# Hybrid three-branch layer: half of a projection's finishing work moved behind the next half, gate tiles in buffers of their own, branch weights asked for earlier

## The chip, the cores and the metric

The kernel runs on one core of one Trainium2 chip. The metric is device time in microseconds (us) of one execution; the median of three runs is taken. TensorE does the matrix products, VectorE (DVE), ScalarE (ACT) and GpSimd (POOL) do the elementwise work, SyncE (SP) and GpSimd issue transfers. Each engine works off its own list of instructions strictly in order, so an instruction that waits holds up everything behind it on its engine, and a transfer that waits in SP's list holds up all later transfers of that list.

## The reference

The layer works on x (1024 rows, width 1024) and 256 memory tokens. After a norm, one wide projection of h gives the inputs of three token mixers (A: top-256 sparse attention, B: low-rank attention, M: attention into the memory), three gate paths z and three merge gates. What matters here is the end of it:

```python
ys = jnp.stack([o_a * jax.nn.silu(z_a), o_b * jax.nn.silu(z_b), o_m * jax.nn.silu(z_m)], axis=0)
branch = jnp.einsum('nbsw,nwd->nbsd', ys, w_branch[layer])
gates = jax.nn.sigmoid(gate_logits)
merged = jnp.einsum('bsnd,nbsd->bsd', gates, branch)
x = x + merged @ w_out[layer]
```

and, for mixer A, the projections q_a, k_a, v_a with a per-head norm and rotary embedding.

## The kernel before

Every product of two fp32 matrices is done as three TensorE products (`mm3`: high by high, high by low, low by high), where high is the operand rounded for TensorE and low the remainder. So each weight block is loaded raw (one transfer on SP's list), its high part is cast on ScalarE and its low part subtracted on VectorE (`wload` and `wsplit`).

The order in time is: memory attention, B's attention, the indexer of A, then branch 2 (M), branch 1 (B), the last projections for A, A's attention, branch 0 (A) and the output projection. A search for the 256th largest index value of each row (`topk_group`; its operations are named `ka..` and `kd..`) is cut into small steps that `run_topk` puts between other work on ScalarE and VectorE, from the indexer to just before A's attention.

`branch(n, ...)` has a first part that makes `y` = mixer output times silu(z), and a merge loop over 8 blocks `d` of 128 output columns, each with two halves `j` of 512 rows: 16 half tiles of 12 matmuls. A half tile needs the block's weights (`b{n}w{d}`), a stored gate tile `tg` (tanh of half the gate logit, computed earlier, stored in HBM and loaded here), and a PSUM bank (names `br`), taken in turn from a group of two and a group of three banks. `emit` then merges: for branches 2 and 1 one VectorE instruction (tg + 1) * br into a tile `ac` (named `ab` for branch 2, `am` for branch 1), which POOL's list sends to HBM, for branch 1 as an accumulating transfer. For branch 0, `emit_a` multiplies, adds the sum from HBM on POOL, casts the high part on ScalarE (`hTh`) and subtracts the low part on VectorE (`hTl`), the inputs of the output projection, whose weights are `wo`.

Between the two parts of branches 2 and 1 stands `qkv(p)` (`mid`): the q, k and v projection of two heads, in two halves `j` of four row blocks each (names `a_0..` and `a_1..`). Per half, the results are copied from PSUM, squared and summed (`ss`), POOL turns the sums into factors (`rr`), VectorE applies rotary, POOL multiplies q and k by the factors, q is split, and q, k, v are stored.

In the phase of branches 2 and 1 the tiles xq, xk, xv, their squares, `tg` and `ac` all come in turn from one pool tag `t2k` with nine buffers; weight tiles share two raw buffers and seven split ones:

```python
return wk.tile([P, 512], F32, tag="t2k", name=nm, bufs=9)
```

A scheduler turns the program into the engines' lists; a buffer's next user waits for its last reader.

Of the kernel before, what the change touches and what calls it, by code (L numbers as in the profile page):

```python
# [11 lines left out]
F32 = mybir.dt.float32  # L12
# [9 lines left out]
S = 1024  # L22
D = 1024
P = 128
# [17 lines left out]
NZG = 3  # L42
WSF = [1]
WSO = [1]
WOD = (1, 1)
ZB5 = 4
OB5 = 4
PRF = (2, 2)
# [47 lines left out]
def f(ap):  # L96
    return ap.bitcast(F32)
# [3 lines left out]
def hybrid_kernel(  # L101
# [922 lines left out]
    def topk_group(ts, nm, act):  # L1024
# [56 lines left out]
        if act:  # L1081
            up = tk.tile([P, nb], F32, name=nm + "u")
            for i, t in enumerate(ts):
                n = (t + 1) * P
                sg = sign(i, t)
                big = tk.tile([P, S], BF, tag="tke", name=f"{nm}b{t}", bufs=1)[:, 0:n]
                nc.vector.tensor_scalar(out=big, in0=sg, scalar1=0.5, scalar2=-GONE, op0=ALU.is_le, op1=ALU.mult)
                y = tk2[0].tile([P, S], F32, tag="tks", name=f"{nm}y{t}", bufs=1)[:, 0:n]
                nc.vector.tensor_tensor_reduce(out=y, in0=idx[t], in1=big, op0=ALU.add, op1=ALU.min, scale=1.0,
                                               scalar=-GONE, accum_out=up[:, i:i + 1])  # L1090
                yield n / 480 + 0.2
            nc.vector.tensor_scalar(out=cnt, in0=cnt, scalar1=TOPK - 0.5, scalar2=None, op0=ALU.is_gt)
            nc.vector.tensor_tensor(up, up, cnt, op=ALU.mult)
            nc.vector.tensor_scalar(out=cnt, in0=cnt, scalar1=-1.0, scalar2=1.0, op0=ALU.mult, op1=ALU.add)
            nc.vector.tensor_tensor(T, T, cnt, op=ALU.mult)
            nc.vector.tensor_tensor(T, T, up, op=ALU.subtract)
            fix[0] = 1
        else:
            nT = tk.tile([P, nb], F32, name=nm + "m")
            nc.vector.tensor_scalar(out=nT, in0=T, scalar1=-1.0, scalar2=None, op0=ALU.mult)  # L1100
# [181 lines left out]
            bg(zi[0], 5.1)  # L1282
        z_done.add((n, w))

    def branch(n, zc, wpool, wk, yp, o_T, emit, bg=None, tgb=9, wkt=None, zb=2, ob=2, mid=None, tgt="t2k"):

        yh, yl, b0 = [None] * 4, [None] * 4, None

        def b_weights(d):
            return wload(wpool, f"b{n}w{d}", [(wview(w_branch[n], 0, 4, d * P, P), P)], 4, P, wkind[1])  # L1290

        early_z = {}
        if n == 0:
            for w in range(4):
                if (n, w) not in z_done:
                    early_z[w] = z_part(n, w, zc, wpool, wk, zb)
            b0 = b_weights(0)
# [36 lines left out]
    with w3s as ph:  # L1334
# [3 lines left out]
        wk = ph.enter_context(tc.tile_pool(name="gwork", bufs=2, reuse_waits="tile"))  # L1338

        def t2k(nm):  # L1340
            return wk.tile([P, 512], F32, tag="t2k", name=nm, bufs=9)

        def acc_at(d, j):
            return s_acc[d * P:(d + 1) * P, j * 512:(j + 1) * 512]

        def emit_b(d, j, tg, pb):
            ac = t2k(f"ab{d}_{j}")
            i_ = nc.vector.scalar_tensor_tensor(out=ac, in0=tg, scalar=1.0, in1=pb, op0=ALU.add, op1=ALU.mult)
            nc.gpsimd.dma_start(acc_at(d, j), ac)
            run_topk(i_, 2.6)  # L1350

        def emit_m(d, j, tg, pb):
            ac = t2k(f"am{d}_{j}")
            i_ = nc.vector.scalar_tensor_tensor(out=ac, in0=tg, scalar=1.0, in1=pb, op0=ALU.add, op1=ALU.mult)
            nc.gpsimd.dma_start(acc_at(d, j), ac, accum_op=ALU.add)
            run_topk(i_, 2.6)

        def qkv(p):
# [9 lines left out]
            for j in range(2):  # L1368
# [8 lines left out]
                for i in range(4):  # L1377
# [7 lines left out]
                    for e, x_ in enumerate((xq, xk, xv)):  # L1385
                        i_ = nc.scalar.copy(x_[:, i], psv[:, e])
                    run_topk(i_, 4.2)
                for e, x_ in enumerate((xk, xq)):
                    sq = t2k(f"{nm}sq{e}").rearrange("p (t d) -> p t d", t=8)
                    nc.scalar.activation(sq, x_.rearrange("p t h d -> p (t h) d"), AF.Square)  # L1390
                    nc.vector.tensor_reduce(out=ss[:, e, :], in_=sq, op=ALU.add, axis=AX.X)  # L1391
                    nc.vector.tensor_tensor(x_.rearrange("p t h d -> p (t h) d"), x_.rearrange("p t h d -> p (t h) d"),
                                            g_am[:, 1 - e:2 - e, :].to_broadcast([P, 8, 64]), op=ALU.mult)
                rsqrt_mean(rr, ss, 1.0 / 64)
                nc.gpsimd.tensor_scalar(out=rr[:, 1, :], in0=rr[:, 1, :], scalar1=64 ** -0.5,
                                        scalar2=0.0, op0=ALU.mult, op1=ALU.add)
                for e, x_ in enumerate((xk, xq)):
                    rope(x_[:, :, :, 0:16], cos_a[:, b, :], sin_a[:, b, :], 2, 8, wk, f"ar{p}_{j}_{e}")
                    r_ = rr[:, e, :].rearrange("p (t h) -> p t h", t=4).unsqueeze(3).to_broadcast([P, 4, 2, 64])
                    nc.gpsimd.tensor_tensor(x_, x_, r_, op=ALU.mult)  # L1400
                nc.scalar.copy(vst[:, :, 0::3, :], xv)
                nc.vector.tensor_tensor(vst[:, :, 1:3, :], xv, f(vst[:, :, 0::3, :]), op=ALU.subtract)
                nc.scalar.copy(qs[:, :, :, 0, :], xq)
                nc.vector.tensor_tensor(qs[:, :, :, 1, :], xq, f(qs[:, :, :, 0, :]), op=ALU.subtract)
                nc.gpsimd.dma_start(s_va[p][j], f(vst).rearrange("p t e d -> p (t e d)"))
                nc.gpsimd.dma_start(s_ka[p][j], xk.rearrange("p t h d -> p (t h d)"))
                nc.gpsimd.dma_start(s_qa[p][j], f(qs).rearrange("p t h e d -> p (t h e d)"))
            return last

        hds = ExitStack()  # L1410
# [18 lines left out]
        def early(a, b):  # L1429
            for w in range(a, b):  # L1430
                z_early(0, w, C_ZA, wpool, wk, run_topk)

        branch(2, C_ZM, wpool, wk, yp, s_om, emit_b, run_topk, ob=2, mid=lambda: qkv(0))
        branch(1, C_ZB, wpool, wk, yp, s_o[1], emit_m, run_topk, ob=2, mid=lambda: qkv(1))
# [113 lines left out]


    with ExitStack() as ph:  # L1550
        wo = [None, None]

        def wo_load(pool, c):
            wo[c] = [wload(pool, f"wo{c}_{kp}", [(wview(w_out, 2 * kp, 2, c * 512, 512), 512)], 2, 512)
                     for kp in range(4)]

        wpa = ph.enter_context(tc.tile_pool(name="w6a", bufs=1, reuse_waits="tile"))
        with ExitStack() as ph2:
# [5 lines left out]
            def emit_a(d, j, tg, pb):  # L1564
# [23 lines left out]
            wkind[1] = ("wb", 6, 512)  # L1588

            ws[:] = WSF  # L1590
            branch(0, C_ZA, wpool, wkz, yp, s_o[0], emit_a, None, 4, wk, ZB5, OB5, tgt="tg")
            ws[:] = WSO
            split_low(None)

# [43 lines left out]
```

## Time and profile before

| | |
|---|---|
| median of 3 runs | 1438.72 us (1437.82 to 1439.06) |
| the profiled execution's own time | 1442.87 us |
| its span, first to last instruction | 1441.1 us |
| TensorE busy | 1366.4 us (95%) |
| VectorE / ScalarE / GpSimd busy | 956.4 / 692.7 / 222.8 us |
| mean granted TensorE clock | 0.988 |

TensorE's clock has two levels; 1.00 in a stretch is 2.4 GHz, 0.50 is 1.2 GHz. A stretch of 100 us of span is 6.9% of it, so an engine's busy share over the span says little about a stage of 60 us; the rows further down are read stage by stage.

### The profile page before, as it was taken

Reading aid. Unit: us, or ns where it says so; the run is one execution under the profiler, and the core shown is the slowest. Engines: PE = TensorE matmul, PEld = TensorE weight load, DVE = VectorE, ACT = ScalarE, POOL = GpSimd, SP = SyncE. Lnnn points to the kernel's source line nnn. Section 1 sums busy time; section 2 is a strip of 40 time slices with the busy share of each in tenths; the row PEclk is TensorE's granted clock in tenths of the full one; section 3 lists DMA queues with packets and bytes.
Section 4 is the critical chain, followed back from the end, with each engine's and each line's share of the span. In section 5 each row is a group of like instructions: output and inputs, shape, how many; then the busy total and the mean of one; then the engine's idle time right before and its main releaser. Section 6 shows DMA issues by size and latency. Waiting matters only on the chain.

```text
span 1441.1 us, 20833 instructions
## 1 busy us (share of the span) xinstructions
PE 1366.4 (95%) x7440; PEld 1169.4 (81%) x7440; DVE 956.4 (66%) x2338; ACT 692.7 (48%) x1520; POOL 222.8 (15%) x248
## 2 busy tenths in 40 slices
PE   7999999999999999999998998889999999997998
PEld 5998888788988889877896787679978888875787
DVE  5845436678888851688866686567768888857411
ACT  6635433366666651455653565333346666543200
POOL 3150004510102000000032004213230000004200
PEclk9999999999999999999999999899999999999999
DMA  7411212311121130111416432872462441266522
GB/s 246 132 45 59 92 37 85 117 52 41 49 73 35 45 126 23 33 41 59 132 53 212 141 107 85 177 177 81 132 197 67 125 132 52 67 222 198 178 96 73
DMA packets 154711, 147.45 MB, mean 102 GB/s; under 512 B 38000, under 2 KB 114800, under 8 KB 154608
## 3 DMA queue, kind: packets, MB, share of 16 engines
q1 hardware_dynamic: 147024, 123.58, 28.9%
q0 software_dynamic: 7008, 20.45, 4.9%
q10 hardware_dynamic: 576, 2.10, 0.4%
q8 instruction: 58, 0.95, 0.3%
q14 instruction: 45, 0.37, 0.1%
HBM read 99.43 MB, written 46.66 MB: 101 GB/s over the span
## 4 chain that ended last, share of the span: by engine, by line
PE 61%; DVE 15%; ACT 7%; DMA 7%; issue 6%; POOL 2%; SPq 1%; DVEq 0%; POOLq 0%; ACTq 0%
PE f L274 6%; PE f L275 5%; PE f L276 5%; DVE kdj L1040 3%; PE o L275 2%; PE o L276 2%; PE o L274 2%; DMA tg<-s_tg 2%; ACT kag L1046 2%; DVE idx L1234 1%; PE ixps L275 1%; PE ixps L276 1%; PE ixps L274 1%; PE b_3pt L463 1%; PE qmps L276 1%
## 5 line engine op out<-in xcount | busy, mean ns | idle before, releaser
L1046 ACT ACTIVATE kag<-idx,kaT 128x896 bf16<-128x896 f32 (+2 forms) x96 | 83.1, 866 | 67.1 <-DVE kaT L1067 64.7
L1040 DVE TENSOR_SCALAR_CACHE_REDUCE kdj<-idx,kdT 128x1024 bf16<-128x1024 f32 (+2 forms) x96 | 92.6, 964 | 1.1
L274 PE MATMUL f<-hTh,f_0h 128*128 128x512 f32 x184 | 78.8, 428 | 3.1 <-ACT fo L366 1.3
L274 PE MATMUL f<-hTh,f_1h 128*128 128x512 f32 x184 | 76.1, 413 | 0.0
L275 PE MATMUL f<-hTl,f_1h 128*128 128x512 f32 x184 | 74.3, 404 | 0.0
L276 PE MATMUL f<-hTh,f_0l 128*128 128x512 f32 x184 | 74.2, 403 | 0.0
L276 PE MATMUL f<-hTh,f_1l 128*128 128x512 f32 x184 | 73.9, 402 | 0.0
L275 PE MATMUL f<-hTl,f_0h 128*128 128x512 f32 x184 | 73.7, 401 | 0.0
L1569 POOL TENSOR_TENSOR ac<-ac,tg 128x512 f32<-128x512 f32 x16 | 26.5, 1667 | 260.0 <-DVE tg L1567 243.4
L1608 DVE TENSOR_TENSOR xr<-o,xr 128x512 f32<-128x512 f32 x16 | 11.1, 692 | 65.2 <-PE o L276 65.2
L366 ACT ACTIVATE fo<-f 128x512 f32<-128x512 f32 x48 | 28.8, 600 | 35.7 <-PE f L276 31.9
L1228 ACT ACTIVATE irl<-is 128x512 f32<-128x512 f32 (+1 forms) x80 | 37.8, 527 | 15.6 <-DVE idx L1234 11.9
L274 PEld LDWEIGHTS f<-hTh,f_0h 128*128 128x128 f32 x184 | 35.0, 190 | 9.7 <-ACT fo L366 2.9
L1234 DVE SCALAR_TENSOR_TENSOR idx<-irl,wi,idx 128x1024 f32<-128x1024 f32 (+5 forms) x42 | 40.3, 959 | 2.7 <-ACT irl L1228 1.0
L276 PEld LDWEIGHTS f<-hTh,f_0l 128*128 128x128 f32 x184 | 35.0, 190 | 6.8
L276 PEld LDWEIGHTS f<-hTh,f_1l 128*128 128x128 f32 x184 | 34.7, 188 | 5.9
L275 PEld LDWEIGHTS f<-hTl,f_1h 128*128 128x128 f32 x184 | 34.8, 189 | 4.3
L274 PEld LDWEIGHTS f<-hTh,f_1h 128*128 128x128 f32 x184 | 34.8, 189 | 4.2
L275 PEld LDWEIGHTS f<-hTl,f_0h 128*128 128x128 f32 x184 | 35.1, 191 | 3.6
L1226 PE MATMUL is<-kih,iqT 128*128 128x512 f32 (+1 forms) x80 | 30.1, 381 | 2.9 <-ACT irl L1228 2.6
L233 POOL TENSOR_SCALAR a_0rr<-a_0ss 128x16 f32<-128x16 f32 x4 | 3.7, 930 | 171.2 <-DVE a_0ss L1391 171.2
L1175 DVE TENSOR_SCALAR wi<-ixps 128x8 f32<-128x8 f32 x8 | 1.3, 167 | 42.0 <-ACT xi L1173 42.0
(1246 smaller groups left out, 4804.9 us busy)
## 6 DMA issues: line engine op xcount, KB each, us to landing
s_tg<-fo SPq DMA_DIRECT2D x48, 256.0 KB, 2.1
tg<-s_tg SPq DMA_DIRECT2D x48, 256.0 KB, 4.2
f_0r<-in_w_in_dram SPq DMA_DIRECT2D x23, 256.0 KB, 3.2
f_1r<-in_w_in_dram SPq DMA_DIRECT2D x23, 256.0 KB, 3.0
xx<-in_x_dram SPq DMA_DIRECT2D x8, 512.0 KB, 7.1
osb<-s_o SPq DMA_DIRECT2D x16, 256.0 KB, 3.1
s_acc<-ab POOLq DMA_DIRECT2D x16, 256.0 KB, 3.6
s_acc<-am POOLq DMA_DIRECT2D x16, 256.0 KB, 5.2
```

The lines of the kernel that those rows point to most:

```text
L274: nc.tensor.matmul(ps, ah, bh, start=start, stop=False)
L275: nc.tensor.matmul(ps, ah, bl, start=False, stop=False)
L276: nc.tensor.matmul(ps, al, bh, start=False, stop=stop)
L366: nc.scalar.activation(o, ps, AF.Tanh, scale=0.5)
L463: nc.tensor.transpose(tp[:, i, :], Pt[b][:, kt * P:(kt + 1) * P], ident)
L1040: nc.vector.tensor_scalar(out=junk, in0=idx[t], scalar1=T[:, i:i + 1], scalar2=0.0, op0=ALU.is_ge, op1=ALU.add, accum_out=cnt[:, i:i + 1])
L1046: nc.scalar.activation(junk, idx[t], AF.Sign, bias=T[:, i:i + 1], accum_out=cnt[:, i:i + 1])
L1226: nc.tensor.matmul(sp[:, 0:w], q_, kih[:, k0:k0 + w], start=True, stop=False)
L1228: nc.scalar.activation(rl[:, k0:k0 + m], sp[:, 0:m], AF.Relu)
L1234: i_ = nc.vector.scalar_tensor_tensor(out=acc[:, 0:n], in0=rl[:, 0:n], scalar=wc, in1=acc[:, 0:n], op0=ALU.mult, op1=ALU.add)
L1569: nc.gpsimd.tensor_tensor(ac, ac, tg, op=ALU.add)
L1608: nc.vector.tensor_tensor(xr, ps, xr, op=ALU.add)
```

## The change

Four things change. In `qkv`, the work from the factors on (scaling of q and k, the split of q, the stores of k and q) is put into a closure `scaled`, which `catch_up()` runs later: for the first half in the middle of the second half, for the second half in the first block of the merge loop; k is scaled on VectorE instead of POOL; v's split and store come earlier. `tg` gets a tag of its own with three buffers, the squares one buffer, and `t2k` shrinks from nine to six. `branch` asks for the weights of up to two blocks ahead. In branch 0, the four pieces of `wo`'s first half are asked for one by one in blocks 2 to 5 instead of all at once in block 1.

```diff
-    def branch(n, zc, wpool, wk, yp, o_T, emit, bg=None, tgb=9, wkt=None, zb=2, ob=2, mid=None, tgt="t2k"):
+    def branch(n, zc, wpool, wk, yp, o_T, emit, bg=None, tgb=3, wkt=None, zb=2, ob=2, mid=None):
...
-            bh, bl = b0 if d == 0 and b0 is not None else b_weights(d)
+            while len(wb) < min(d + 3, NK):
+                wb.append(b_weights(len(wb)))
+            bh, bl = wb[d]
             for j in range(2):
-                tg = (wkt or wk).tile([P, 512], F32, tag=tgt, name=f"tg{n}_{d}_{j}", bufs=tgb)
+                tg = (wkt or wk).tile([P, 512], F32, tag="tg", name=f"tg{n}_{d}_{j}", bufs=tgb)
...
-            return wk.tile([P, 512], F32, tag="t2k", name=nm, bufs=9)
+            return wk.tile([P, 512], F32, tag="t2k", name=nm, bufs=6)
+        behind = []
+        def catch_up():
+            while behind:
+                behind.pop()()
...
         def emit_b(d, j, tg, pb):
             ac = t2k(f"ab{d}_{j}")
+            if j:
+                catch_up()
...
                     run_topk(i_, 4.2)
+                    if i == 1:
+                        catch_up()
...
-                    sq = t2k(f"{nm}sq{e}").rearrange("p (t d) -> p t d", t=8)
+                    sq = wk.tile([P, 8, 64], F32, tag="asq", name=f"{nm}sq{e}", bufs=1)
...
+                nc.scalar.copy(vst[:, :, 0::3, :], xv)
+                nc.vector.tensor_tensor(vst[:, :, 1:3, :], xv, f(vst[:, :, 0::3, :]), op=ALU.subtract)
+                nc.gpsimd.dma_start(s_va[p][j], f(vst).rearrange("p t e d -> p (t e d)"))
                 for e, x_ in enumerate((xk, xq)):
                     rope(x_[:, :, :, 0:16], cos_a[:, b, :], sin_a[:, b, :], 2, 8, wk, f"ar{p}_{j}_{e}")
-                    nc.gpsimd.tensor_tensor(x_, x_, r_, op=ALU.mult)
...
+                def scaled(p=p, j=j, xq=xq, xk=xk, rr=rr, qs=qs):
+                    for e, eng, x_ in ((1, nc.gpsimd, xq), (0, nc.vector, xk)):
+                        r_ = rr[:, e, :].rearrange("p (t h) -> p t h", t=4).unsqueeze(3).to_broadcast([P, 4, 2, 64])
+                        eng.tensor_tensor(x_, x_, r_, op=ALU.mult)
+                    nc.gpsimd.dma_start(s_ka[p][j], xk.rearrange("p t h d -> p (t h d)"))
+                    nc.scalar.copy(qs[:, :, :, 0, :], xq)
+                    nc.vector.tensor_tensor(qs[:, :, :, 1, :], xq, f(qs[:, :, :, 0, :]), op=ALU.subtract)
+                    nc.gpsimd.dma_start(s_qa[p][j], f(qs).rearrange("p t h e d -> p (t h e d)"))
+                behind.append(scaled)
...
-                if (d, j) == WOD:
+                if d > 1 and j and d < 6:
                     pool_raw[:] = [1, 8]
-                    wo_load(wpa, 0)
+                    wo_load(wpa, 0, [d - 2])
```

TensorE's list is the same before and after. The other lists move. On SP's list, around branch 2's merge loop, before (`b2w` are weight blocks, `tg_d_j` gate tiles, `osb` the first operand of branch 1):

```order
L258 DMA b2w4r<-in_w_branch_dram 128x4x128
L1305 DMA osb_0_1_8905<-s_o_96 128x512
L1323 DMA tg_0_0_8407<-s_tg_101 128x512
L1323 DMA tg_0_1_8427<-s_tg_101 128x512
L258 DMA b2w5r<-in_w_branch_dram 128x4x128
L1323 DMA tg_1_0_8460<-s_tg_101 128x512
L258 DMA b2w6r<-in_w_branch_dram 128x4x128
L1323 DMA tg_1_1_8484<-s_tg_101 128x512
```

and with the change, at the same place:

```order
L257 DMA b2w4r<-in_w_branch_dram 128x4x128
L1304 DMA osb_0_1_8905<-s_o_96 128x512
L1324 DMA tg_1_1_8496<-s_tg_101 128x512
L1324 DMA tg_2_0_8522<-s_tg_101 128x512
L257 DMA b2w5r<-in_w_branch_dram 128x4x128
L1324 DMA tg_2_1_8549<-s_tg_101 128x512
L1324 DMA tg_3_0_8579<-s_tg_101 128x512
L257 DMA b2w6r<-in_w_branch_dram 128x4x128
```

The first three gate tiles now stand some twenty rows earlier, among the loads of branch 2's first part, and each weight block has three more gate tiles ahead of it; branch 1 is changed in the same way. On VectorE's list at the start of branch 2's merge loop, before (`ar` rows are rotary, `kdj` and `kar` search steps):

```order
L1040 TENSOR_SCALAR kdj_8425,kdc<-idx_6263,kdT 128x768
L244 TENSOR_TENSOR b2w3l<-b2w3r,b2w3h 128x512
L1348 SCALAR_TENSOR_TENSOR ab_1_8442<-tg_0_1_8427,br_0_1_8429 128x512
L1404 TENSOR_TENSOR a_1qs<-a_1xq,a_1qs 128x8x64
L1065 TENSOR_TENSOR kac<-kac,kan 128x3
```

and with the change:

```order
L1420 TENSOR_TENSOR a_1xk<-a_1xk,a_1rr 128x512
L426 TENSOR_TENSOR a_1xq<-ar_1_1rp_8385,ar_1_1rp_8386 128x8x8
L427 TENSOR_TENSOR a_1xq<-ar_1_1rp_8387,ar_1_1rp_8388 128x8x8
L1358 SCALAR_TENSOR_TENSOR ab_1_8448<-tg_0_1_8433,br_0_1_8435 128x512
L1064 TENSOR_TENSOR kac<-kac,kan 128x3
L243 TENSOR_TENSOR b2w3l<-b2w3r,b2w3h 128x512
L1065 TENSOR_SCALAR kar<-kac 128x3
L1358 SCALAR_TENSOR_TENSOR ab_0_8487<-tg_1_0_8472,br_1_0_8474 128x512
L1423 TENSOR_TENSOR a_1qs<-a_1xq,a_1qs 128x8x64
```

The second merge moved ahead of the weight subtraction, the scaling of k stands ahead of both, and the split of q behind one more merge. On SP's list in branch 0's merge loop, before (`ac` is the sum loaded from HBM):

```order
L258 DMA wo_2r<-in_w_out_dram 128x2x512
L1566 DMA ac_0_14213<-s_acc 128x512
L1566 DMA ac_1_14234<-s_acc 128x512
L1566 DMA ac_0_14261<-s_acc 128x512
L1323 DMA tg_4_1_14267<-s_tg_99 128x512
L1323 DMA tg_5_0_14294<-s_tg_99 128x512
L1323 DMA tg_5_1_14315<-s_tg_99 128x512
L258 DMA wo_3r<-in_w_out_dram 128x2x512
L1566 DMA ac_1_14282<-s_acc 128x512
L1566 DMA ac_0_14309<-s_acc 128x512
L258 DMA b0w6r<-in_w_branch_dram 128x4x128
```

and with the change:

```order
L257 DMA wo_1r<-in_w_out_dram 128x2x512
L1585 DMA ac_1_14174<-s_acc 128x512
L1324 DMA tg_3_1_14213<-s_tg_99 128x512
L257 DMA b0w6r<-in_w_branch_dram 128x4x128
L1585 DMA ac_0_14207<-s_acc 128x512
L1585 DMA ac_1_14228<-s_acc 128x512
L1324 DMA tg_4_0_14246<-s_tg_99 128x512
L1324 DMA tg_4_1_14267<-s_tg_99 128x512
L1585 DMA ac_0_14261<-s_acc 128x512
L257 DMA wo_2r<-in_w_out_dram 128x2x512
```

The weight block `b0w6` moved from behind the fourth `wo` piece to behind the second, ahead of gate tile (4,0).

## Rows read from the trace of the kernel before

**Rows 1.** The page: busy time of TensorE.

```profile
PE 1366.4 (95%) x7440; PEld 1169.4 (81%) x7440; DVE 956.4 (66%) x2338; ACT 692.7 (48%) x1520; POOL 222.8 (15%) x248
```

**Rows 2.** Waits of PE over the span: total us, times, longest us.

```profile
PE br L274 <- DVE am L1354: 12.4, 5, 4.7
PE br L274 <- ACT b0w6h L241: 8.6, 1, 8.6
PE br L274 <- DVE ab L1348: 8.5, 4, 4.0
```

**Rows 3.** Windows, `br` matmuls alone, first to next stage's first: branches 2, 1, 0.

```profile
core 0: us, PE busy (x), PEclk, DMA share, GB/s
743.28:799.14 55.86, 47.36 (x192) 0.97 0.55 181
881.21:948.36 67.15, 50.40 (x192) 0.91 0.74 175
1287.43:1347.60 60.17, 47.99 (x192) 0.91 0.65 205
```

**Rows 4.** Timeline of PE: first and twelfth matmul of a half tile.

```profile
881.21 0.40 PE L274 MATMUL br<-yh,b1w0h 128*128 128x512 f32 x1
...
883.77 0.40 PE L276 MATMUL br<-yh,b1w0l 128*128 128x512 f32 x1
```

**Rows 5.** Timeline of SP's list in branch 1: start, us of issuing, transfer.

```profile
896.79 0.56 SPq L1323 DMA_DIRECT2D tg<-s_tg  x1
902.59 0.38 SPq L258 DMA_DIRECT2D b1w6r<-in_w_branch_dram  x1
903.02 1.08 SPq L1323 DMA_DIRECT2D tg<-s_tg  x2
```

**Rows 6.** Timeline of VectorE in branch 1: start, us, [idle before <- releaser].

```profile
901.84 0.68 DVE L244 TENSOR_TENSOR b1w4l<-b1w4r,b1w4h 128x512 fp32r<-128x512 f32 x1
...
909.28 0.69 DVE L1354 SCALAR_TENSOR_TENSOR am<-tg,br 128x512 f32<-128x512 f32 x1 [5.22 <-DMA tg<-s_tg]
```

**Rows 7.** Timeline at branch 2's start: weight subtractions on VectorE, scaling on POOL.

```profile
755.48 3.02 DVE L244 TENSOR_TENSOR b2w3l<-b2w3r,b2w3h 128x512 fp32r<-128x512 f32 x1
...
769.86 0.69 DVE L244 TENSOR_TENSOR b2w5l<-b2w5r,b2w5h 128x512 fp32r<-128x512 f32 x1
...
755.88 1.06 POOL L1400 TENSOR_TENSOR a_1xk<-a_1xk,a_1rr 128x512 f32<-128x512 f32 x1
756.89 1.05 POOL L1400 TENSOR_TENSOR a_1xq<-a_1xq,a_1rr 128x512 f32<-128x512 f32 x1
```

**Rows 8.** Transfers issued in 881.21 to 948.36: count, KB each, median us to landing.

```profile
tg<-s_tg SPq DMA_DIRECT2D x14, 256.0 KB, 6.1
s_acc<-am POOLq DMA_DIRECT2D x13, 256.0 KB, 5.7
```

**Rows 9.** Timeline in branch 0: SP's list, ScalarE and PE around weight block 6.

```profile
1324.39 0.38 SPq L258 DMA_DIRECT2D wo_3r<-in_w_out_dram  x1
...
1326.09 0.42 SPq L258 DMA_DIRECT2D b0w6r<-in_w_branch_dram  x1
...
1331.82 0.60 ACT L241 CAST b0w6h<-b0w6r 128x512 fp32r<-128x512 f32 x1
...
1332.47 0.79 PE L274 MATMUL br<-yh,b0w6h 128*128 128x512 f32 x1 [8.61 <-ACT b0w6h L241]
```

**Rows 10.** Branch 0's additions (page) and loads of the sum (1287.43 to 1347.60).

```profile
L1569 POOL TENSOR_TENSOR ac<-ac,tg 128x512 f32<-128x512 f32 x16 | 26.5, 1667 | 260.0 <-DVE tg L1567 243.4
...
ac<-s_acc SPq DMA_DIRECT2D x14, 256.0 KB, 4.5
```

**Rows 11.** Timeline: POOL makes the factors of a second half (branch 1).

```profile
892.47 2.92 POOL L234 TENSOR_TENSOR a_1rr<-a_1rr,mhalf 128x16 f32<-128x16 f32 x1
```

**Rows 12.** Timeline of VectorE: the search's last step, and the first masked scores.

```profile
1038.91 0.22 DVE L1117 TENSOR_TENSOR idx<-idx,cmask 128x128 bf16<-128x128 bf16 x1
...
1063.72 0.69 DVE L491 CUSTOM_DVE_ANT_0 a_3p<-a_3S,idx 128x512 f32<-128x512 f32 x1 [0.88 <-PE a_3S L1519]
```

More of the change, by code (lines that the diff above doesn't have):

```diff
@@ L44 @@
 WSO = [1]
-WOD = (1, 1)
 ZB5 = 4
@@ L1087, in topk_group @@
                 nc.vector.tensor_scalar(out=big, in0=sg, scalar1=0.5, scalar2=-GONE, op0=ALU.is_le, op1=ALU.mult)
-                y = tk2[0].tile([P, S], F32, tag="tks", name=f"{nm}y{t}", bufs=1)[:, 0:n]
+                y = tk2[0].tile([P, 7 * P], F32, tag="tks", name=f"{nm}y{t}", bufs=1)[:, 0:n]
                 nc.vector.tensor_tensor_reduce(out=y, in0=idx[t], in1=big, op0=ALU.add, op1=ALU.min, scale=1.0,
@@ L1283, in z_early @@
         z_done.add((n, w))
-    def branch(n, zc, wpool, wk, yp, o_T, emit, bg=None, tgb=9, wkt=None, zb=2, ob=2, mid=None, tgt="t2k"):
-        yh, yl, b0 = [None] * 4, [None] * 4, None
+    def branch(n, zc, wpool, wk, yp, o_T, emit, bg=None, tgb=3, wkt=None, zb=2, ob=2, mid=None):
+        yh, yl, wb = [None] * 4, [None] * 4, []
         def b_weights(d):
@@ L1296, in branch @@
                     early_z[w] = z_part(n, w, zc, wpool, wk, zb)
-            b0 = b_weights(0)
+            wb.append(b_weights(0))
         for w in range(4):
@@ L1353, in emit_m @@
             ac = t2k(f"am{d}_{j}")
+            if j:
+                catch_up()
             i_ = nc.vector.scalar_tensor_tensor(out=ac, in0=tg, scalar=1.0, in1=pb, op0=ALU.add, op1=ALU.mult)
@@ L1387, in qkv @@
                     run_topk(i_, 4.2)
+                    if i == 1:
+                        catch_up()
                 for e, x_ in enumerate((xk, xq)):
-                    sq = t2k(f"{nm}sq{e}").rearrange("p (t d) -> p t d", t=8)
-                    nc.scalar.activation(sq, x_.rearrange("p t h d -> p (t h) d"), AF.Square)
+                    v = x_.rearrange("p t h d -> p (t h) d")
+                    sq = wk.tile([P, 8, 64], F32, tag="asq", name=f"{nm}sq{e}", bufs=1)
+                    nc.scalar.activation(sq, v, AF.Square)
                     nc.vector.tensor_reduce(out=ss[:, e, :], in_=sq, op=ALU.add, axis=AX.X)
-                    nc.vector.tensor_tensor(x_.rearrange("p t h d -> p (t h) d"), x_.rearrange("p t h d -> p (t h) d"),
-                                            g_am[:, 1 - e:2 - e, :].to_broadcast([P, 8, 64]), op=ALU.mult)
+                    nc.vector.tensor_tensor(v, v, g_am[:, 1 - e:2 - e, :].to_broadcast([P, 8, 64]), op=ALU.mult)
                 rsqrt_mean(rr, ss, 1.0 / 64)
@@ L1431, in early @@
                 z_early(0, w, C_ZA, wpool, wk, run_topk)
+                catch_up()
         branch(2, C_ZM, wpool, wk, yp, s_om, emit_b, run_topk, ob=2, mid=lambda: qkv(0))
@@ L1550, in hybrid_kernel, with wo_load @@
     with ExitStack() as ph:
[L1551 to L1555, printed above, removed]
+        wo = [[], []]
+        def wo_load(pool, c, kps=range(4)):
+            wo[c] += [wload(pool, f"wo{c}_{kp}", [(wview(w_out, 2 * kp, 2, c * 512, 512), 512)], 2, 512)
+                      for kp in kps]
         wpa = ph.enter_context(tc.tile_pool(name="w6a", bufs=1, reuse_waits="tile"))
@@ L1590, in hybrid_kernel @@
             ws[:] = WSF
-            branch(0, C_ZA, wpool, wkz, yp, s_o[0], emit_a, None, 4, wk, ZB5, OB5, tgt="tg")
+            branch(0, C_ZA, wpool, wkz, yp, s_o[0], emit_a, None, 4, wk, ZB5, OB5)
             ws[:] = WSO
```

8 lines of the change are left out of this document (removed).

## The prediction

> **What bounds the kernel now.** I began with the page's busy times. TensorE is busy 1366.4 us of a span of 1441.1 [rows 1]; its instructions do not change, so only its idle time and its slow-clock time, some 75 us of span, can be won or lost. Next I read its waits for those at the change's place. Three groups stand out: 12.4 us for VectorE's merges of branch 1 (`am`), 8.6 for the cast of branch 0's weight block 6, and 8.5 for the merges of branch 2 (`ab`) [rows 2]. All fall in the three merge loops, so I read each loop as a window: 55.86, 67.15 and 60.17 us for branches 2, 1 and 0, at granted clocks of 0.97, 0.91 and 0.91 [rows 3].
>
> What a loop would take if nothing held TensorE follows from the distance of the first and the twelfth matmul of a half tile: 883.77 − 881.21 = 2.56 us for eleven steps, 2.79 for twelve, and 16 half tiles take 44.7 us [rows 4]. The losses against that are 11.2, 22.5 and 15.5 us, in all 49.2. Each has two parts. Idle time is window minus busy: 8.5, 16.75 and 12.2. Busy time above 44.7 is the slow clock that follows an idle stretch: 2.7, 5.7 and 3.3 [rows 3]. So an idle microsecond costs up to 1.3.
>
> TensorE may run some three half tiles ahead of the merges, since five banks take turns; a merge stops it when it is later than about 3 × 2.79 = 8.4 us. What makes it so late? In branch 1, the issue list shows two gate tiles issued at 903.02, right behind weight block 6 at 902.59, and the issue before that at 896.79 [rows 5]. Block 6 waits for a raw buffer, which block 4's subtraction gives back at 901.84 + 0.68 = 902.52 [rows 6]. The gate tile then takes 6.1 us to land [rows 8], and the merge at 909.28 has stood idle 5.22 us for it [rows 6]. So: subtraction late, weight load late, gate tile behind it late, merge late, TensorE stopped. In branch 0 the fourth `wo` piece is issued at 1324.39, block 6 only at 1326.09, its cast runs at 1331.82, and TensorE goes on at 1332.47 after 8.61 us [rows 9]. In branch 2 the list of VectorE (the change section) has weight block 3 ahead of the second merge; that subtraction takes 3.02 us where block 5's takes 0.69, and POOL scales k and q in that time [rows 7].
>
> **The change, part by part.** *Branch 2.* The second merge no longer stands behind that subtraction, and the next gate tiles are asked for before the weights. I leave 1.2 us for the one scaling still on POOL (half of 3.02 − 0.69 = 2.33) and 0.8 for the start of the loop, where VectorE's scaling of k may wait for the factors. Loss 11.2 to 2: **gain 9.2**. The bounds are 0 (another merge takes the late one's place) and 11.2.
>
> The Trainium skill bears on this ("SBUF — State Buffer", Who interferes with whom): VectorE's second pair of ports is GpSimd's only pair, under an exclusive lock. The trace agrees: 3.02 against 0.69 us [rows 7]. By that rule, k's scaling on VectorE, which reads two tiles, is itself shut out while POOL scales q, so moving it wins only one POOL pass and the gain would be about 1 us smaller in each of two loops.
>
> *The scaling of k on VectorE* is four instructions; I price one as a subtraction of the same 512 columns, 0.69 us [rows 7], off TensorE's path while merges have their 8.4 us of cover. Its wait for the factors is bounded by nothing and by the 2.92 us of POOL's power [rows 11]; the rotary steps stand ahead of it, so I take at most half. Behind it in the list are the second merge and weight block 3; neither comes near 8.4. The first half's scaling and stores move into the projection's second half, where TensorE waits for none of them. The second half's stores of k and q now stand in POOL's list ahead of later `ac` stores; the cover is `t2k`'s buffers, three of six being free for `ac` until xk goes, and three merges give 8.4 us against a landing of 5.7 [rows 8]. If that cover were gone, a merge would wait for a buffer by the difference, 1 to 3 us. I count nothing.
>
> *Branch 1.* With three buffers of its own, gate tile i is asked for once merge i − 3 is done. The loop back is issue 1.08 / 2 = 0.54 [rows 5], landing 6.1 [rows 8] and merge 0.69 [rows 6], 7.3 us in three half tiles, under the 8.4 that TensorE needs for them: short, but enough. Then the transfers limit. Their share is 0.74 of 67.15 us, 49.7 us of work for all engines together; three of the loop's gate loads move ahead of it, 0.75 MB at 175 GB/s [rows 3] over 0.74, which is 3.2 us, leaving 46.5, above the 44.7 of TensorE. At a share of 0.9, my choice between today's 0.74 and full, this takes 51.7 us, so 7.0 remains lost, and 1.2 as in branch 2 for POOL's scaling. Loss 22.5 to about 8: **gain 14.5**. The bounds: at today's share 46.5 / 0.74 = 62.8, a gain of 4.4; none, if the landing grows past 7.2 us (8.4 less 0.54 and 0.69); 22.5 if nothing binds.
>
> *Weights two blocks ahead.* This adds no load and no buffer: raw and split tiles are as many as before, so a load still waits for the subtraction that frees its buffer, and asking sooner does little by itself. It counts inside the two gains.
>
> *Branch 0.* With the `wo` pieces spread, block 6 is asked for behind the second piece instead of the fourth, and the 8.61 us wait goes [rows 2, 9]. What then paces the loop is the sum from HBM: landing 4.5, addition 1.67 [rows 10], a cast priced as block 6's 0.60 [rows 9] and a subtraction as 0.69 [rows 7], together 7.5 us for three buffers against 8.4. The other idle time, 12.2 − 8.6 = 3.6, stays, and 1.4 of the 3.3 of slow clock with it. Loss 15.5 to 5: **gain 10.5**. The bounds are 0 (a later piece holds the list as the fourth does) and 15.5.
>
> *The sum* is 9.2 + 14.5 + 10.5 = 34.2 us. From the profiled execution's own 1442.87 this makes 1408.7; that execution is 4.15 above the median of the runs, 1438.72, so for a median I predict **1404.5 us**.
>
> **The rivals.** *Transfers keep branch 1 as it is:* its share stays near 0.74 and its gain is 0 to 4.4, which gives 1415 to 1419. For it: a share that high and gate tiles that land in 6.1 us, beside accumulating stores in 5.7 [rows 8]. Against it: 11 of its 16.75 idle us have nothing in the DMA rows to explain them but the order of the list. By the Trainium skill ("DMA: Bandwidth & Descriptors", Issuing engines are not separate DMA queues) everything runs on the same 16 engines, so asking sooner gives no bandwidth; branch 1 is where the trace could show it, branch 2 with 0.55 [rows 3] is not.
>
> *The search collects what the loops win.* Its steps are placed between the merges; if it, and not TensorE, must be done for mixer A's attention to begin, the 23.7 us of branches 2 and 1 are given back there, and only branch 0's 10.5 stay: 1428. Against it: 24.8 us lie between the search's last step at 1038.91 and the first masked scores at 1063.72 [rows 12], which is more than 23.7, but only just.
>
> *All is recovered:* 49.2 less than before, about 1390.
>
> *The other side:* with only three gate buffers, a gate tile that waits for its merge now holds SP's list itself, and weights stand behind it. One such hold is priced by block 6's: 8.61 idle and 3.3 of slow clock [rows 2, 3], 12 us. Up to two leave a gain; the third makes 36 against 34.2, and the kernel ends at 1441 or more. For it: the changed list has three gate tiles ahead of each weight block. Against it: weights now asked for two blocks ahead have 4 × 2.79 = 11 us of cover.
>
> *It does nothing:* the held weight load only changes its place, and each loop keeps its loss.
>
> **How the numbers follow.** The forecast has 0.58, with a range of its own of 1396 to 1412; transfers in branch 1 0.20; the search 0.08; all recovered 0.08; slower 0.04; nothing 0.02. The range of 1391 to 1424 leaves out slower, nothing, most of the search's case, and the lower end of "all recovered". Faster by over 0.2% (2.9 us, about what a measurement of this kernel can tell from no change) is 0.58 + 0.20 + 0.08 + 0.08 = 0.94.
>
> **What the changed profile would show.** Right: the three windows at about 47, 53 and 50 us with clocks of 0.97 or more; no wait of TensorE for `b0w6h`; under 3 us in all for `ab`, and under 8 for `am`; in branch 1 a DMA share of 0.85 to 0.9; subtractions at branch 2's start under 2 us. The branch 1 term is wrong if its window stays over 60 us at a share of 0.74 or with tiles that land later than 7.2; the branch 2 term if `ab` still waits over 5; the branch 0 term if another `wo` or weight block ends a wait of several us. If the windows shrink and the time doesn't, the stretch before mixer A's attention has grown, and the search is the cause. A wait of SP's list at gate tiles, with weight casts ending TensorE's waits, would show the slower side.

## The result, and the profile after

The changed kernel takes 1401.06 us (median of 4 runs, 1400.65 to 1402.0) against 1438.27 for the kernel before in the same series: a ratio of 0.9743, 95% interval 0.9726 to 0.9760, or 37 us less. The profiled executions differ by a little more, 1441.1 − 1400.2 = 40.9 us of span. Stage by stage, from the first matmul of a stage to the first of the next:

| us | before | after | difference |
|---|---|---|---|
| branch 2's merge loop | 55.86 | 45.17 | −10.7 |
| between the loops (z and projection) | 82.07 | 78.58 | −3.5 |
| branch 1's merge loop | 67.15 | 47.50 | −19.7 |
| on to A's attention | 108.52 | 109.14 | +0.6 |
| A's attention and z | 230.55 | 229.54 | −1.0 |
| branch 0's merge loop | 60.17 | 47.12 | −13.1 |
| output projection, to the end | 93.50 | 99.57 | +6.1 |

The page's busy times, where [rows 1] stood; TensorE's busy time fell by 8 us though its instructions are the same, which fits slow clock gone: the granted clock of the three loops, further down, went from 0.97, 0.91 and 0.91 to 1.00.

```profile
PE 1358.3 (97%) x7440; PEld 1167.8 (83%) x7440; DVE 957.9 (68%) x2346; ACT 693.4 (50%) x1520; POOL 213.7 (15%) x240
```

TensorE's waits, where [rows 2] had 12.4, 8.6 and 8.5 us for the three loops. Of those, one wait of 1.7 is left, the last line; the first two lines are waits at new places:

```profile
PE a L274 <- DVE a3w3l L243: 4.3, 1, 4.3
...
PE o L273 <- ACT hTh L1589: 2.0, 1, 2.0
...
PE br L273 <- DVE am L1366: 1.7, 1, 1.7
```

The three loops as windows of the `br` matmuls (us, busy, granted clock, share of the DMA engines, GB/s), in the order of [rows 3], branches 2, 1 and 0. The clock is 1.00 in all three:

```profile
743.58:788.75 45.17, 45.05 (x192) 1.00 0.70 233
867.33:914.83 47.50, 45.22 (x192) 1.00 0.85 210
1253.51:1300.63 47.12, 44.98 (x192) 1.00 0.75 237
```

SP's list in branch 1, where [rows 5] had a gate tile behind `b1w6r`, 6.2 us after the one before it. Weight blocks 5, 6 and 7 are now issued 4.6 and 3.4 us apart; before, the same three stood at 896.31, 902.59 and 911.13, 6.3 and 8.5 apart, where a block gives TensorE 2 × 2.79 = 5.6 us of work:

```profile
882.73 0.38 SPq L257 DMA_DIRECT2D b1w5r<-in_w_branch_dram  x1
883.36 2.12 SPq L1324 DMA_DIRECT2D tg<-s_tg  x2
887.33 0.38 SPq L257 DMA_DIRECT2D b1w6r<-in_w_branch_dram  x1
888.42 0.46 SPq L1324 DMA_DIRECT2D tg<-s_tg  x1
890.70 0.38 SPq L257 DMA_DIRECT2D b1w7r<-in_w_branch_dram  x1
```

The transfers issued in that loop land no sooner than in [rows 8] (6.1 and 5.7 there). They are asked for sooner:

```profile
tg<-s_tg SPq DMA_DIRECT2D x13, 256.0 KB, 6.2
s_acc<-am POOLq DMA_DIRECT2D x13, 256.0 KB, 6.5
```

Single tiles still land late. The one issued at 888.42 landed 10.7 us later, VectorE's merge waited for it, and TensorE's 1.7 us come right behind that merge:

```profile
899.22 0.69 DVE L1366 SCALAR_TENSOR_TENSOR am<-tg,br 128x512 f32<-128x512 f32 x1 [0.44 <-DMA tg<-s_tg]
```

The 6.1 us that are given back lie at the start of the output projection. TensorE reaches `hTh` and `hTl` of the last block before they are there, and then runs slowly: a matmul behind the waits takes 0.63 us instead of 0.40 [rows 4], and the window that follows has a granted clock of 0.77, so a part of it was at the lower of the two levels:

```profile
1307.64 0.50 PE L273 MATMUL o<-wo_3h,hTh 128*128 128x512 f32 x1 [1.98 <-ACT hTh L1589]
...
1309.22 0.79 PE L275 MATMUL o<-wo_3h,hTl 128*128 128x512 f32 x1 [0.85 <-DVE hTl L1601]
1309.81 0.63 PE L273 MATMUL o<-wo_0h,hTh 128*128 128x512 f32 x1
```

```profile
1310.63:1320.63 10.00, 10.00 (x35) 7.95 (x34) 3.26 (x4) 2.50 (x3) 0.00 (x0) 0.77 0.69 230
```

### The profile page after: what moved, and what is told of

The parts are those of the page before. It is cut to its first block, busy times and chain, and to the rows that moved or that the text cites. A ratio compares the mean times of both kernels' runs of the same rounds, so it can differ in the third digit from the quotient of the medians.

```text
span 1400.2 us, 20838 instructions
## 1 busy us (share of the span) xinstructions
PE 1358.3 (97%) x7440; PEld 1167.8 (83%) x7440; DVE 957.9 (68%) x2346; ACT 693.4 (50%) x1520; POOL 213.7 (15%) x240
## 4 chain that ended last, share of the span: by engine, by line
PE 67%; DVE 13%; ACT 6%; DMA 4%; issue 4%; POOL 3%; SPq 1%; DVEq 0%; ACTq 0%; POOLq 0%
PE f L273 6%; PE f L274 5%; PE f L275 5%; DVE kdj L1039 3%; PE o L275 2%; PE o L273 2%; PE o L274 2%; PE br L273 2%; PE br L275 2%; PE br L274 2%; ACT kag L1045 2%; DVE idx L1233 1%; PE ixps L274 1%; PE ixps L275 1%; PE ixps L273 1%
## 5 line engine op out<-in xcount | busy, mean ns | idle before, releaser
L1045 ACT ACTIVATE kag<-idx,kaT 128x896 bf16<-128x896 f32 (+2 forms) x96 | 83.0, 865 | 43.5 <-DVE kaT L1066 34.2
L1627 DVE TENSOR_TENSOR xr<-o,xr 128x512 f32<-128x512 f32 x16 | 11.1, 691 | 62.4 <-PE o L275 62.3
L1226 PE MATMUL is<-kil,iqT 128*128 128x512 f32 (+1 forms) x80 | 27.5, 354 | 0.0
```

The costliest lines, as they stand in the source:

```text
L1045: nc.scalar.activation(junk, idx[t], AF.Sign, bias=T[:, i:i + 1], accum_out=cnt[:, i:i + 1])
L1226: nc.tensor.matmul(sp[:, 0:w], q_, kil[:, k0:k0 + w], start=False, stop=True)
L1627: nc.vector.tensor_tensor(xr, ps, xr, op=ALU.add)
```

## The experiments

Twelve kernels: four undo one part of the change, three do one part alone, two test the mechanism in the kernel before, one takes a gate buffer away, and two put together what was left. The stages of all, in us (the last column runs from branch 0's first matmul to the end, since what its loop wins can come back as a wait behind it):

| kernel | branch 2 | between | branch 1 | to A | branch 0 to end | ratio to before (95%) |
|---|---|---|---|---|---|---|
| before | 55.9 | 82.1 | 67.2 | 108.5 | 153.7 | |
| the change | 45.2 | 78.6 | 47.5 | 109.1 | 146.7 | 0.9743 (0.9726 to 0.9760) |
| tags undone | 51.4 | 78.6 | 52.1 | 106.0 | 144.7 | 0.9770 (0.9746 to 0.9794) |
| closure undone | 45.0 | 78.3 | 50.3 | 107.1 | 144.0 | 0.9730 (0.9701 to 0.9759) |
| asking ahead undone | 47.8 | 78.6 | 47.2 | 110.7 | 147.3 | 0.9768 (0.9744 to 0.9791) |
| wo spread undone | 45.7 | 78.6 | 49.5 | 109.8 | 144.1 | 0.9742 (0.9723 to 0.9760) |
| tags alone | 47.1 | 78.6 | 48.2 | 108.0 | 154.1 | 0.9807 (0.9790 to 0.9823) |
| closure alone | 51.1 | 78.6 | 51.5 | 106.6 | 152.6 | 0.9822 (0.9807 to 0.9836) |
| asking ahead alone | 55.7 | 82.4 | 66.4 | 105.5 | 143.9 | 0.9924 (0.9904 to 0.9944) |
| two gate buffers | 46.0 | 80.6 | 53.1 | 110.5 | 141.6 | 0.9806 (0.9781 to 0.9832) |
| three raw buffers | 52.5 | 82.6 | 66.3 | 104.7 | 153.7 | 0.9976 (0.9963 to 0.9988) |
| weights on POOL | 48.4 | 78.6 | 61.5 | 105.1 | 153.2 | 0.9881 (0.9865 to 0.9898) |
| tags and ahead | 44.9 | 78.6 | 48.2 | 111.3 | 143.1 | 0.9754 (0.9738 to 0.9771) |
| the same, four sums | 44.8 | 78.3 | 48.0 | 113.5 | 139.6 | 0.9717 (0.9699 to 0.9735) |

Kernels with the same code in a stage differ there by some us (the change and the kernel with two gate buffers share the code of branch 0 to the end: 146.7 and 141.6), so single microseconds of a stage carry nothing. Nor is an edit's effect confined to its own rows, since the scheduler orders all lists anew. One edit of the change is not in the list of its parts: a scratch tile of the search (`y`) is 896 instead of 1024 columns wide. All kernels here have it but those of asking ahead alone and of weights on POOL; its instructions use no more than 896 columns in either kernel.

**Undoing one part.** In the changed kernel, one after the other:

```diff
# undo_tag
-def branch(..., tgb=3, ...):
+def branch(..., tgb=9, ..., tgt="t2k"):
...
-            return wk.tile([P, 512], F32, tag="t2k", name=nm, bufs=6)
+            return wk.tile([P, 512], F32, tag="t2k", name=nm, bufs=9)
...
-                    sq = wk.tile([P, 8, 64], F32, tag="asq", name=f"{nm}sq{e}", bufs=1)
+                    sq = t2k(f"{nm}sq{e}").rearrange("p (t d) -> p t d", t=8)
# undo_closure
-                behind.append(scaled)
+                scaled()
# undo_ahead
-            while len(wb) < min(d + 3, NK):
+            while len(wb) < d + 1:
# undo_wo
-                if d > 1 and j and d < 6:
+                if (d, j) == (1, 1):
...
-                    wo_load(wpa, 0, [d - 2])
+                    wo_load(wpa, 0)
```

> The changed kernel (1401.1 us) with the gate tiles, the squares and the merged tiles in one tag of nine buffers again; the other three parts stay. Theory: the buffers of its own are what lets a gate tile be asked for as soon as merge i-3 is done, so most of branch 1's gain and part of branch 2's go: 1401 + 8 to 15 = 1409 to 1416 us, with waits of TensorE for am back at 5 us or more. Rival: the order of VectorE's list (the closure) did it, and the tags do nothing: 1400 to 1403 us.

> The changed kernel with the scaling, the split of q and the stores of k and q run at once again, k's scaling still on VectorE. Theory: branch 2's gain came from the second merge standing ahead of work that waits for POOL, so ab waits come back: branch 2's window 45.2 to about 52, branch 1's 47.5 to about 51, in all 1409 to 1414 us. Rival: the tags and the early gate tiles did it, and the order at the loop's start hides in TensorE's lead of three half tiles: within 2 us of 1401.

> The changed kernel with each block's weights asked for at its own block again. Theory: nothing, since a raw buffer decides when a load can start and the scheduler's list moves by one gate tile per block only: 1400 to 1403 us. Rival: asking ahead is what takes weight loads out from in front of the gate tiles; without it branch 1's share of transfers falls under 0.80 and its window is over 52 us: 1406 us or more.

> The changed kernel with all four pieces of wo asked for in block 1 of branch 0 again. Theory: weight block 6 or 7 waits behind them, an 8 to 9 us wait of TensorE for its cast and 3 us of slow clock come back, and the output projection's start recovers at most its 6 us, since the tail of the sums is no longer late: 1404 to 1409 us. Rival 1: weights asked for two blocks ahead already pull block 6 out from behind the pieces, and the early pieces free the tail: 1395 to 1399 us, faster than the change. Rival 2: all 13 us of branch 0's loop come back: 1413 us.

Medians 1407.39, 1399.70, 1406.12 and 1402.59 us, beside 1440.01 of the kernel before. The tags' theory holds in the windows (51.4 and 52.1 us, one `am` wait of 5.3), but the time lost is under its 8 to 15 us: the two loops lose 10.8, and later stages give half of that back. The closure's theory falls for branch 2, which is as short without it, and the time is within 2 us of the change; branch 1 does come near its 51 us (50.3), but undoing the spread of `wo`, which leaves the code there alone, makes 49.5 of it. For asking ahead, the theory of no effect fails in branch 0, where TensorE waits again for block 6's cast:

```profile
PE br L273 <- ACT b0w6h L240: 5.4, 1, 5.4
```

That makes the loop 6.7 us longer, and nearly all of it comes back behind it (147.3 us from branch 0 to the end, 146.7 with the change). So the 1406 us, the rival's number, don't come from there, nor from branch 1, as the rival had it (47.2 us); in the trace 2.7 us more lie in branch 2 and 1.6 before A's attention, too little to be told from the spread between kernels. For wo the theory falls too, and its first rival holds in part: block 6 needs no spread, but the tail wins too little to be told from the change. No undoing costs more than 0.3%, by the centres of the intervals, where all four together win 2.6%. So the parts stand in for each other.

**One part alone**, from the kernel before (the closure with k's scaling on VectorE and v's early store, the tags with the squares' buffer):

> The kernel before with the buffer tags alone changed (gate tiles three buffers of their own, squares one, six left for the rest); scaling at once on POOL, weights and wo as before. Theory: in branches 2 and 1 the gate tiles asked for early carry most of the gain, as each of the other parts could be undone at 0 to 5 us: branch 2's window 55.9 to 48 to 51, branch 1's 67.2 to 50 to 54, 3 us more in the stage between; branch 0 as before with its 8.6 us wait: 1438 - 20 to 26 = 1412 to 1418 us. Rival: the parts stand in for each other, and the tag alone leaves the merges behind the subtraction that POOL stretches: branch 2 stays over 54, 1425 us or more.

> The changed kernel with the tags, the asking ahead and the wo pieces as before: only the late scaling, k's scaling on VectorE and v's early store are left. Theory: the second merge no longer stands behind POOL, which with the shared tag gave windows of 51.4 and 52.1 us for branches 2 and 1 where weights were asked ahead; so 51 to 53 each, branch 0 as before: 1438 - 18 to 24 = 1414 to 1420 us. Rival: without its own tag a gate tile still stands behind the held weight load, and branch 1 keeps most of its 12 us of am waits: over 60 us there, 1428 us or more.

> The kernel before with only the asking two blocks ahead. SP's list then differs from that of before in branch 0 alone, where block 6 stands ahead of the third wo piece. Theory: the 8.6 us wait for block 6 goes, and with the sums' tail some 7 us of the 13 of that loop stay won; branches 2 and 1 keep 55.9 and 67.2: 1430 to 1433 us. Rival: block 6 needs the wo pieces spread as well, 1436 us or more.

Medians 1411.53, 1413.16 and 1428.60, beside 1439.01, each a little under its theory's range. From branch 2 to the end of branch 1, the tags alone win nearly all and the closure alone most of what the change wins: 8.8 + 3.5 + 18.9 = 31.2 us, and 4.8 + 3.5 + 15.7 = 24.0, where the whole change wins 10.7 + 3.5 + 19.7 = 33.9. Together the two would make 55.2, so they don't add up. The windows, of the tags alone and then of the closure alone (branches 2, 1, 0); branch 0 keeps its slow clock in both:

```profile
744.85:791.90 47.05, 45.60 (x192) 1.00 0.70 229
870.48:918.71 48.23, 45.21 (x192) 1.00 0.82 206
1256.83:1317.39 60.56, 48.19 (x192) 0.89 0.64 205
```

```profile
743.25:794.36 51.11, 47.34 (x192) 0.93 0.67 222
872.94:924.39 51.45, 47.12 (x192) 0.93 0.87 212
1260.36:1319.52 59.16, 47.23 (x192) 0.88 0.64 206
```

Asking ahead alone touches neither of those branches and wins 9.8 us from branch 0 to the end. SP's list there has block 6 ahead of the third piece, with every piece still asked for in block 1:

```profile
1307.61 0.38 SPq L258 DMA_DIRECT2D b0w6r<-in_w_branch_dram  x1
1308.28 0.38 SPq L258 DMA_DIRECT2D wo_2r<-in_w_out_dram  x1
```

**Is it the place behind the weight load, or the buffer?** Two kernels from the one before, with tags, closure and the rest as they were:

```diff
# raw_three (t2k 8 instead of 9)
-                    pool_raw[:] = [2, 8, 768]
+                    pool_raw[:] = [3, 8, 768]
# weights_on_pool: the loads of b2w and b1w
-            last_load[0] = nc.sync.dma_start(raw[:, :, o:o + w], ap)
+            last_load[0] = (q or nc.sync).dma_start(raw[:, :, o:o + w], ap)
```

> The kernel before with three raw weight buffers instead of two in branches 2 and 1 (one shared buffer less for gate, merged and projection tiles, 8 instead of 9). Tags, closure, asking ahead and wo as before. Theory: a weight load that waits for a raw buffer holds the gate tiles behind it; with a third buffer the load no longer waits for a late subtraction, so the gate tiles are issued on time: branch 2 to 47 to 51 us, branch 1 to 50 to 56, in all 1414 to 1424 us. Rival: a gate tile waits for its own buffer, which it shares with merged tiles that come free only when their store has landed; then a third raw buffer does nothing, and the eighth instead of ninth shared buffer makes it worse: 1438 to 1445 us with am and ab waits of 20 us or more.

> The kernel before with the weight loads of branches 2 and 1 issued from POOL's list instead of SP's; tags, closure, asking ahead and wo as before, and every other row of SP's list in the same order but for a few gate tiles beside z weights. Theory: a gate tile is late because it stands in SP's list behind a weight load that waits for its raw buffer; with no such load in that list, branch 2 goes to 47 to 51 us and branch 1 to 50 to 56 with am and ab waits under 6 us in all: 1414 to 1424 us. Rival: the gate tile waits for one of the nine shared buffers, and the place of the weight load does nothing: both windows stay within 3 us, 1433 to 1440 us, with SP's list still waiting at gate tiles for projection or merged tiles; a weight load held in POOL's list can make it slower still.

1435.32 beside 1438.86 us, and 1422.21 beside 1440.06. For the third raw buffer neither range holds: 0.2% faster, where the rival had it no faster and the theory by 14 us at least. It fails as a remedy: the scheduler asks for weights one block further ahead again, so that a held load stands in front of the gate tiles as before. SP's waits in branches 2 and 1 (us, times, longest):

```profile
SPq L258 <- DVE b2w3l L244: 13.2, 1, 13.2
SPq L258 <- DVE b1w3l L244: 9.8, 1, 9.8
...
SPq L258 <- DVE b1w7l L244: 8.4, 1, 8.4
```

With the branch weights out of SP's list the time is in the theory's range, and branch 2 wins 7.5 us, as the theory has it, but branch 1 only 5.6; the two loops' waits for merges are 11.1 us, not under 6. In branch 2 the second merge still stands behind the subtraction that POOL stretches:

```profile
755.58 3.02 DVE L244 TENSOR_TENSOR b2w3l<-b2w3r,b2w3h 128x512 fp32r<-128x512 f32 x1
758.52 0.68 DVE L1348 SCALAR_TENSOR_TENSOR ab<-tg,br 128x512 f32<-128x512 f32 x1
```

What holds the rest of branch 1 is of the same kind: other weight loads. SP's list and the merge on VectorE in branch 1 of that kernel:

```profile
902.86 0.38 SPq L258 DMA_DIRECT2D z0w_0r<-in_w_in_dram  x1
903.34 2.32 SPq L1323 DMA_DIRECT2D tg<-s_tg  x3
```

```profile
910.10 0.69 DVE L1354 SCALAR_TENSOR_TENSOR am<-tg,br 128x512 f32<-128x512 f32 x1 [6.20 <-DMA tg<-s_tg]
```

The load of `z0w_0` waited 11.4 us for the raw buffer of `b1w6`, 7.8 until that block had landed and 3.6 until it was subtracted; the gate tile came right behind it, and the merge waited 6.20. The same list also waits four times, 3.0 to 7.8 us, at gate tiles for projection tiles of the shared tag. So the place behind a held load is shown as the cause for most of branch 2 and a part of branch 1, and the shared buffers hold beside it; their shares in branch 1 weren't parted further.

**How few gate buffers will do?** The changed kernel with `bufs=2` for the gate tiles of branches 2 and 1:

> The changed kernel with two gate buffers instead of three in branches 2 and 1. Theory: the loop back of issue 0.54, landing 6.2 and merge 0.69 is 7.4 us for two half tiles, 3.7 each against 2.79, so branch 1's window becomes 58 to 62 us and branch 2's (landing 5.2) 51 to 54: 1401 + 17 to 21 = 1418 to 1422 us, with SP's list held at gate tiles. Rival: with fewer transfers under way a gate tile lands in some 3 to 4 us (2.1 to 3.9 elsewhere in the trace), the loop back is 5 us for 5.6, and nothing happens: 1400 to 1405 us.

1411.17 beside 1439.01 us. Neither fits: the sizes are far below the theory's in branch 2 (46.0 against 51 to 54) and below in branch 1 (53.1 against 58 to 62). The landing gave way, as the rival had it, from 6.2 to 4.6 us in branch 1 and from 5.2 to 4.2 in branch 2:

```profile
tg<-s_tg SPq DMA_DIRECT2D x13, 256.0 KB, 4.6
```

With these, the loop back is 0.54 + 4.2 + 0.69 = 5.4 us in branch 2, under the 5.6 of two half tiles, and 5.8 in branch 1, just over. This fits the sign in both; 0.2 us in eight turns is not the 5.6 that branch 1 lost. In the trace one late merge, 31 us into the loop, stops TensorE for 3.5 us, two others for 0.7 to 1.1, and the granted clock is 0.97. The trace is of the quickest of four executions (1407.12 us; the slowest took 1415.21), so the loss in the others may lie elsewhere.

**What is needed, and what is left.** The kernel before with the two parts that the runs had singled out, and then with a fourth buffer for branch 0's sums:

```diff
-                ac = wk.tile([P, 512], F32, tag="ac", name=f"ac{d}_{j}", bufs=3)
+                ac = wk.tile([P, 512], F32, tag="ac", name=f"ac{d}_{j}", bufs=4)
```

> The kernel before with two of the four parts: the tags, and weights asked for two blocks ahead. Scaling at once on POOL, wo all in block 1. Theory: these two carry the whole gain, 27.5 us (branches 2 and 1 and the stage between, as with the tags alone) and 9.8 us (branch 0 to the end, as with asking ahead alone): 1438.5 - 37 = 1401 us, 1399 to 1404. Rival: the closure and the spread of wo each add what the single undoing hid: 1405 us or more.

> As the kernel with tags and asking ahead, with four instead of three buffers for branch 0's sums loaded from HBM. Theory: what is left of branch 0's loss lies in the chain of load, addition, cast and subtraction over three buffers, which ends some 3 us late for the output projection and costs slow clock there: 4 to 6 us less than with three, 1395 to 1397 us, the output projection 93.5 us and no wait of TensorE for hTh or hTl. Rival: VectorE's list, with the splits of wo and of the weights between the merges, sets that chain; then four buffers change under 1.5 us.

1402.09 and 1397.11 us, beside 1438.86, the first in its theory's range, the second at the edge of it. The two parts give the change's time within the intervals. The fourth buffer gives 5.0 us more by the medians; its interval (0.9699 to 0.9735) lies below that of three buffers (0.9738 to 0.9771). In the two traces the output projection takes 97.2 us with three buffers and 93.8 with four. With three TensorE waits 1.2 us there for `hTh` and 0.4 for `hTl`; with four it has these waits left from branch 0 to the end, and none for the sums:

```profile
PE br L274 <- ACT yh L1310: 0.9, 2, 0.5
PE br L275 <- DVE yl L1311: 0.2, 1, 0.2
```

## Why the prediction was right, and where its steps were not

The forecast of 1404.5 us missed by 3.4, and its sum of 34.2 against 40.9 of the two executions came out of the right stages, though not always by the step named. That it comes so close is in part luck: the 3.5 us by which branch 0 fell short and the 3.5 us between the loops, which it didn't count, cancel. The 75 us that it gives as all that can be won are idle time alone; slow clock lies in the busy time, and 8 us of the win came from there.

*Branch 1, 14.5 forecast, 19.7 measured.* The mechanism was right: gate tiles asked for late, not bandwidth. Asked for early, with the tags alone, they bring 18.9 us. The prediction put their lateness to the place behind the weight load alone; taking the branch weights out of the list brings 5.6, and what of the rest is the shared buffers stays open. The mis-sized term is the transfers' work, 46.5 us. It was 0.85 × 47.50 = 40.4, since the shorter loop also moved less: 10.0 MB by 210 GB/s, where 175 × 67.15 makes 11.75, with five loads of the next projection's weights inside instead of nine (0.5 MB of that). The share of 0.85 is the low end of the 0.85 to 0.9 forecast, and the rival of a share that stays at 0.74 is refuted. The Trainium skill's sentence on the 16 common engines ("DMA: Bandwidth & Descriptors", Issuing engines are not separate DMA queues) isn't contradicted by that: the engines had room, and 0.74 was a loop that waited, not engines that were full.

*Branch 2, 9.2 forecast, 10.7 measured, by the wrong step.* "The second merge no longer stands behind that subtraction" was to bring it. With the weights on POOL's list the merge still stands there, behind 3.02 us of subtraction, and the loop takes 48.4 us; with the closure alone it stands ahead, and the loop takes 51.1, TensorE stopped once for 3.8 us by a merge that had waited for its gate tile. So the late gate tile was most of the cause here too. The tags alone, with both scalings on POOL and run at once, leave 47.1, but with them the scheduler puts the second merge ahead of the subtraction as well. What makes the parts stand in for each other is a circle in the rows: a late merge holds the weight subtraction behind it on VectorE, this holds the raw buffer, that the weight load, and the load the next gate tile, which makes the next merge late. One round in the kernel before follows [rows 5, 6], the merge at 909.28 first:

```profile
910.41 0.69 DVE L244 TENSOR_TENSOR b1w5l<-b1w5r,b1w5h 128x512 fp32r<-128x512 f32 x1
...
911.13 0.38 SPq L258 DMA_DIRECT2D b1w7r<-in_w_branch_dram  x1
911.68 0.96 SPq L1323 DMA_DIRECT2D tg<-s_tg  x2
...
917.07 0.69 DVE L1354 SCALAR_TENSOR_TENSOR am<-tg,br 128x512 f32<-128x512 f32 x1 [3.70 <-DMA tg<-s_tg]
918.61 0.69 DVE L244 TENSOR_TENSOR b1w6l<-b1w6r,b1w6h 128x512 fp32r<-128x512 f32 x1
```

So a slip at the start of branch 1's loop goes round, with 6.3 to 8.5 us between weight loads where TensorE needs one every 5.6. The tags cut the circle between load and tile. That this cut pays is shown by the weights moved to POOL, for most of branch 2 and a part of branch 1. How the closure helps stays open: with it alone a late merge still stops TensorE once in each loop (3.8 and 4.3 us), but isn't passed on, and branch 1's weight loads stand 3.5 to 5.5 us apart.

*The lock between VectorE and POOL* was priced right and paid elsewhere. In the changed kernel k's scaling took 0.69 us on VectorE behind 0.52 us of waiting for the factors, not shut out, since POOL's pass on q began only at 758.11, and that pass stretched a search step that takes 0.16 elsewhere:

```profile
756.24 0.69 DVE L1420 TENSOR_TENSOR a_1xk<-a_1xk,a_1rr 128x512 f32<-128x512 f32 x1 [0.52 <-POOL a_1rr L233]
...
757.72 1.48 DVE L1064 TENSOR_TENSOR kac<-kac,kan 128x3 f32<-128x3 f32 x1
```

That is 1.3 us lost beside one pass of 1.06 and 2.33 in [rows 7] beside two; the same `kac` step beside two passes, with the tags alone, loses 2.2:

```profile
758.92 2.39 DVE L1065 TENSOR_TENSOR kac<-kac,kan 128x3 f32<-128x3 f32 x1
```

The Trainium skill's rule ("SBUF — State Buffer", Who interferes with whom) agrees with all three. But none of it reached TensorE once merges were on time: the 1.2 us put into each loop for it were not there.

*Branch 0, 10.5 forecast, 7.0 measured (13.1 won in the loop, 6.1 given back behind it; 5 us more in the kernel with two gate buffers, which has the same code there), by the wrong part.* The step that failed is "asking sooner does little by itself", with the gain put to the wo pieces: asking ahead alone wins 9.8 us, undoing the spread costs nothing that can be told. Either order takes block 6 out from behind the pieces, and asking ahead does it better (5.4 us of wait are left in the loop where the weights aren't asked for ahead, though to the end that kernel still wins 6.4). The sums' chain, named as what paces the loop (7.5 against 8.4 us), was too slow over three buffers at the loop's end; it showed not as idle time in the loop but as a late last block, and the fourth buffer, which takes it away, shows that the buffers are part of it. What VectorE's list adds was not parted: in the changed kernel's trace the wait for `hTh` goes back to a product of block 7 that stands at 1304.53 behind an `hTl` which waited 1.26 us for its own cast, with a split of `wo` at 1299.23 ahead of both.

*Not counted:* 3.5 us between the loops, where TensorE had waited 2.9 us for subtractions of z weights, and no longer does, once the circle is cut, also with the tags, the closure or the weights on POOL alone. And the search did collect a little, though not as the rival had it: in the stage before A's attention TensorE now waits 4.3 us for the subtraction of `a3w3`, and that stage takes 106 to 114 us in the kernels with short loops against 105 in three of the four with a long branch 1. VectorE works without a pause for 4.8 us before that subtraction, at search steps and at the projection's own finishing work; that the search delays it is argued, not shown.

*The other side* didn't come: SP's list does wait at gate tiles, up to 36.1 us at once, but for the fourth tile of a loop, asked for long before its merge can run.

## What to carry to other kernels

When a transfer lands late, look at what stands ahead of it on the issuing list and what that waits for, and follow it until the chain closes: here a late merge delayed its own successor through VectorE's list, a raw buffer and SP's list, and either of two parts alone was worth most of the gain in those loops. Test parts of a change alone as well as undone, since parts that stand in for each other all look worthless when undone. And follow a stage's gain past its end: a loop that runs ahead of its tail shows the tail as a wait in the next stage.

## What the runs showed of the hardware that was not expected

Gate tiles of 256 KB landed in 6.2 us with three buffers and 4.6 with two in the same loop, at shares of the DMA engines of 0.85 and 0.83: the landing was longer with more tiles asked for at once, so a loop back worked out from the landing with three overstated what two would cost.
